# A two-product Strassen-style MLP kernel on one core: x by a plain load, w1 in five chunks, input checks moved, w2 sums made earlier

## The chip, the core and the metric

The kernel runs on one core of a Trainium2 chip. The metric is the time of one execution on the device in microseconds (us). Kernels are compared by the median of several executions, and by a ratio from rounds in which both ran on the same chip. A ratio is the mean time of one kernel's fast runs over that of the other's fast runs of the same rounds, so it is not quite the ratio of the medians that I quote.

Engines have short names in the profile: PE is TensorE (matrix products), PEld its weight loads, DVE is VectorE, ACT is ScalarE, POOL is GpSimd, SP is the engine that only issues DMA.

## The reference

```python
batch, seq, dim, hidden = 16, 256, 512, 2048      # 4096 tokens, all float32
h = x @ w1                                        # w1: 512 x 4096
gate, value = np.split(h, 2, axis=-1)
h = np.maximum(gate, 0) * value
return h @ w2                                     # w2: 2048 x 512
```

## The kernel before

Both products use Winograd's form of Strassen's algorithm: seven half-size products in place of eight, paid for with sums. For the weights the sums are called T1 to T4, for the data S1 to S4. The 4096 tokens are worked through in four sets of 1024. A set has a first product of 16 blocks (128 hidden columns each) and a second product of four token blocks; the tail of one set overlaps the start of the next. Set 0 makes its first two blocks by ordinary products ("plain"), because the sums are not there yet.

The inputs are cast to f16 while they are loaded. That is only safe for inputs of ordinary size, so ScalarE squares and adds up every part of x, w1 and w2 (a "check", `look` in the code), and a verdict at the end (`judge`, `count`) decides whether a slow, general version must run instead.

One block of the first product. TensorE runs P1, P5, P2, P6, P3, P7 and P4, two matmuls each, interleaved with the next block:

```python
def P1(self):
    self.X = psx.tile(...);  self.mm("P1", self.X, True)
    self.Y = psy.tile(...);  nc.scalar.copy(out=self.Y, in_=self.X)     # Y starts as a copy of X
def P5(self):
    self.W = psw.tile(...);  self.mm("P5", self.W, True)
    nc.scalar.activation(self.p5, self.W, COPY, scale=GS)
def P2(self):
    self.mm("P2", self.X, False)              # must wait until ScalarE has read X
def P6(self):
    self.mm("P6", self.Y, False)              # adds to what ScalarE wrote
    nc.scalar.activation(self.u2, self.Y, COPY, scale=GS)
# ... P3: two VectorE ops; P7: one; P4: one, which writes g
```

The start, the checks and the work around the two products:

```python
# start: everything through GpSimd's casting DMA queue
for b in range(0, NB, 2):
    nc.gpsimd.dma_start(out=xn[:, b:b + 2], in_=x_v[0, :, b:b + 2])    # first half of x, f16
fetch_w1(0)                                                            # w1 of blocks 0 and 1
nc.gpsimd.dma_start(out=xn[:, NB:], in_=x_v[0, :, NB:])                # second half
for i in range(1, 6): fetch_w1(i)                                      # w1 in eight chunks
# ... in set 0 GpSimd makes T1 to T4 of w1, pair of blocks by pair of blocks, then all of w2's,
# then w1's of blocks 0 and 1:
if jb // 2 + 1 < NP: w1_ops(jb // 2 + 1)
else:                w2_ops(); w1_ops(0)
# checks: two of x in a block, or one of w1 (sets 1, 2), or two of x and one of w2 (set 3)
at_block(s, (4 if s == 0 else i // (2 * NB)) + i // 2, look_x)
at_block(1 + i // NP, 8 + i % NP, look_w1);  at_block(3, 1 + i, look_w2);  at_block(3, 13, judge)
# ... after set 0's first product, VectorE makes S1, S2, S4, S3 of g, in two halves each
for m in ("S1", "S2", "S4", "S3"):
    for h in (0, NHC // 2): g_sum(nc.vector, go, m, h, h + NHC // 2)
# second product: two token blocks at a time
for b in range(0, NB, 2):
    for name in ("P1", "P2", "P5", "P6", "P3", "P7", "P4"):
        for c in (b, b + 1): yield from step(name, c)
```

## Time and profile before

| | before |
|---|---|
| median time | 344.91 us (344.87 to 345.13, 3 runs) |
| span of the profiled run | 343.8 us |
| first product of block 2 / its last product | 20.0 / 26.3 us |
| period of a block in the first product | 3.02 to 3.06 us without a check, 3.13, 3.23 and up to 4.31 with checks |
| last product of set 0's last block to the last product of set 1's first | 39.5 us |

First the page of the profile: the span, TensorE's row of busy tenths in 40 slices, and the row of its granted clock in tenths.

```profile
span 343.8 us, 5094 instructions
PE   6889999937999998999999998999997777999993
PEclk9999999987999999999999999999999999999998
```

TensorE is the engine that bounds the kernel, with holes at the start, in slices 9 and 10 (69 to 86 us) and in slices 31 to 34 (258 to 292 us). The clock falls where the second hole is.

Who TensorE waited for (us in total, number of waits, the longest):

```profile
PE X L196 <- ACT Y L203: 11.1, 13, 1.1
PE W L270 <- DVE g_S L261: 7.5, 3, 4.4
PE W L196 <- POOL wt L150: 0.7, 2, 0.5
```

Line 196 is a matmul of the first product, line 270 one of the second. The first wait is P2, which adds to X and must wait until ScalarE has copied X to Y. The second is the second product, waiting for the sums of g.

The chain of waits (start, us, what) shows why the copy is late:

```profile
133.38 0.82 ACT sq L183
134.52 0.50 ACT Y L203
135.06 0.59 PE X L196 x2
```

A check (`sq`) sits on ScalarE right before the copy. The start of every block's last product, read from the timeline, gives what this costs. Against 3.045 us a block (the mean period where there is no check), set 0 loses 1.6 us, sets 1 and 2 lose 2.9 us each, set 3 loses 10.0 us.

The hole at 69 to 86 us, in the timeline of VectorE and of GpSimd (start, us for all, engine, line, operation, output and input, count):

```profile
68.70 7.19 DVE L261 TENSOR_TENSOR g_S<-g 128x2048 f16<-128x2048 f16 x2
75.82 4.26 DVE L261 TENSOR_TENSOR g_S<-g_S,g 128x2048 f16<-128x2048 f16 x2
80.00 4.26 DVE L261 TENSOR_TENSOR g_S<-g,g_S 128x2048 f16<-128x2048 f16 x2
84.19 2.35 DVE L261 TENSOR_TENSOR g_S<-g 128x2048 f16<-128x2048 f16 x2
```

```profile
69.78 5.04 POOL L153 TENSOR_TENSOR v_T<-w_sb,v_T 128x2048 f16<-128x2048 f16 x1
...
81.05 2.13 POOL L150 TENSOR_TENSOR wt<-wr,wt 128x512 f16<-128x512 f16 x1
```

Four pairs of the same size take 7.2, 4.3, 4.3 and 2.35 us. GpSimd is summing w2 and w1 until 83.2 us, and only the last pair is free of it. The Trainium skill, "SBUF — State Buffer", section Who interferes with whom, says why: VectorE and GpSimd share one pair of SBUF ports under an exclusive lock, and a VectorE operation with two SBUF inputs and a GpSimd operation that reads SBUF block each other for a whole instruction. The trace agrees: a sum takes 1.2 us when alone, and beside GpSimd 2.1 us (the second and third pair) or 3.6 us (the mean of the first).

### The profile page before, as it was taken

What the parts mean: (1) busy time and instruction counts of PE and PEld (TensorE: products, weight loads), DVE (VectorE), ACT (ScalarE), POOL (GpSimd) and SP (SyncE); (2) the same over time, 40 slices, a digit from 0 to 9 for tenths busy, and PEclk for the clock granted to TensorE, in tenths of its full rate; (3) what the DMA queues carried; (4) which work ended last, traced back from release to release, by engine and by line L of the source; (5) the groups of instructions that cost most, each with busy time, mean ns of one, the idle gap of its engine ahead of it and who ended that gap; (6) DMA issues with size and microseconds to landing.
All of it is one profiled execution on the core that took longest, in us unless ns stands there. A gap on an engine that the chain in (4) does not pass through costs nothing.

```text
span 343.8 us, 5094 instructions
## 1 busy us (share of the span) xinstructions
PE 311.8 (91%) x1847; PEld 179.8 (52%) x1847; DVE 216.0 (63%) x328; ACT 191.3 (56%) x451; POOL 166.4 (48%) x146
## 2 busy tenths in 40 slices
PE   6889999937999998999999998999997777999993
PEld 2433444615884443448874443458873333436883
DVE  1377788899516886885327887784336565798301
ACT  2347786401238678783338778772348888553230
POOL 8499999996001433992001344991001232698000
PEclk9999999987999999999999999999999999999998
DMA  7999994350320100018320200026220100000113
GB/s 97 192 196 200 227 218 95 61 122 2 122 93 31 61 3 0 0 37 152 121 92 33 61 0 0 2 54 169 85 93 31 61 2 0 1 0 3 64 60 129
DMA packets 32541, 25.54 MB, mean 74 GB/s; under 512 B 13728, under 2 KB 28448, under 8 KB 32416
## 3 DMA queue, kind: packets, MB, share of 16 engines
q0 software_dynamic: 11776, 10.49, 19.2%
q1 hardware_dynamic: 20592, 14.62, 14.5%
q8 instruction: 16, 0.26, 0.3%
q14 instruction: 13, 0.11, 0.1%
q10 hardware_dynamic: 144, 0.07, 0.1%
HBM read 24.12 MB, written 11.53 MB: 104 GB/s over the span
## 4 chain that ended last, share of the span: by engine, by line
PE 62%; ACT 13%; DVE 8%; issue 7%; POOL 6%; DMA 3%; ACTq 0%; DVEq 0%; POOLq 0%
PE Y L196 16%; PE X L196 13%; PE Y L270 11%; PE X L270 8%; PE W L196 8%; PE W L270 7%; ACT sq L183 6%; DVE g_S L261 5%; ACT Y L203 4%; POOL wt L150 3%; DMA wr<-in_w_dram 3%; ACT pu L217 2%; POOL wr L337 2%; DVE cc L223 1%; POOL w_sb L431 1%
## 5 line engine op out<-in xcount | busy, mean ns | idle before, releaser
L261 POOL TENSOR_TENSOR g_S<-g 128x512 f16<-128x512 f16 x42 | 48.5, 1155 | 141.7 <-DVE g L233 141.7
L196 PE MATMUL X<-x_A,wr 128*128 128x512 f16 x248 | 73.6, 378 | 11.8 <-ACT Y L203 11.1
L196 PEld LDWEIGHTS <-wt 128*128 128x128 f16 x496 | 48.0, 97 | 59.5 <-POOL wt L150 2.5
L223 DVE SCALAR_TENSOR_TENSOR cc<-W,pu 128x512 f32<-128x512 f32 x62 | 42.8, 691 | 53.1 <-ACT pu L217 52.9
L196 PE MATMUL Y<-x_S,wt 128*128 128x512 f16 x248 | 73.7, 379 | 0.0
L196 PEld LDWEIGHTS <-wr 128*128 128x128 f16 x372 | 36.1, 97 | 60.9 <-issue 24.6
L270 PEld LDWEIGHTS <-g_S 128*128 128x128 f16 x512 | 50.7, 100 | 16.9 <-DVE g_S L261 10.0
L217 ACT ACTIVATE pu<-Y 128x512 f32<-128x512 f32 x62 | 37.0, 597 | 37.5 <-PE Y L196 37.5
L224 DVE SCALAR_TENSOR_TENSOR g<-X,cc 128x512 f16<-128x512 f32 x62 | 42.9, 691 | 2.4
L233 DVE SCALAR_TENSOR_TENSOR g<-Y,cc 128x512 f16<-128x512 f32 x62 | 42.2, 681 | 2.8 <-PE Y L196 2.8
L229 DVE SCALAR_TENSOR_TENSOR cc<-Y,pu 128x512 f32<-128x512 f32 x62 | 42.2, 681 | 0.3 <-PE Y L196 0.2
L203 ACT COPY Y<-X 128x512 f32<-128x512 f32 x62 | 35.9, 578 | 11.1 <-PE X L196 8.6
L270 PEld LDWEIGHTS <-g 128*128 128x128 f16 x384 | 37.5, 98 | 8.3 <-issue 0.2
L196 PE MATMUL W<-x_S,wr 128*128 128x512 f16 x124 | 36.9, 379 | 0.8 <-DVE x_S L178 0.8
L196 PE MATMUL W<-x_S,wt 128*128 128x512 f16 x124 | 36.9, 380 | 0.7 <-POOL wt L150 0.7
L196 PE MATMUL Y<-x_A,wt 128*128 128x512 f16 x124 | 36.9, 379 | 0.7 <-DVE flag L409 0.7
L210 ACT ACTIVATE pu<-W 128x512 f32<-128x512 f32 x62 | 36.6, 590 | 0.7 <-PE W L196 0.7
L270 PE MATMUL Y<-v_T,g_S 128*128 128x256 f16 x256 | 32.1, 279 | 0.9 <-DVE g_S L261 0.9
L299 DVE SCALAR_TENSOR_TENSOR o<-W,pv 128x256 f32<-128x256 f32 x16 | 6.7, 423 | 40.4 <-PE W L270 19.8
L270 PE MATMUL X<-w_sb,g 128*128 128x256 f16 x256 | 30.6, 273 | 0.0
L319 ACT ACTIVATE o<-Y 128x256 f32<-128x256 f32 x15 | 5.7, 379 | 36.0 <-PE Y L270 36.0
L270 PE MATMUL W<-v_T,g_S 128*128 128x256 f16 x128 | 16.7, 287 | 6.0 <-DVE g_S L261 6.0
(62 smaller groups left out, 327.8 us busy)
## 6 DMA issues: line engine op xcount, KB each, us to landing
out_dram<-o SPq DMA_DIRECT2D x31, 256.0 KB, 2.0
wr<-in_w_dram POOLq DMA_DIRECT2D x16, 256.0 KB, 10.2
x<-in_x_dram POOLq DMA_DIRECT2D x3, 1024.0 KB, 14.9
xn<-x SPq DMA_DIRECT2D x6, 512.0 KB, 4.1
w_sb<-in_w_dram POOLq DMA_DIRECT2D x4, 512.0 KB, 9.5
g_S<-in_x_dram POOLq DMA_DIRECT2D x2, 256.0 KB, 5.0
g_S<-in_x_dram POOLq DMA_DIRECT2D x1, 512.0 KB, 8.9
x_A<-x SPq DMA_TRANSPOSE x12, 3.6
```

The source lines that it names most:

```text
L150: turned(lambda n, a, b, o: nc.gpsimd.tensor_tensor(W[n](i), W[a](i), W[b](i), op=o))
L183: nc.scalar.activation(sq, t, SQUARE, scale=(P / of) ** 0.5, accum_out=st[:, at:at + 1])
L196: nc.tensor.matmul(ps, W[wn](self.jb // 2)[:, b, js], self.xo[xn][:, b, :], start=fresh and b == 0, stop=b == 1, skip_group_check=True)
L203: nc.scalar.copy(out=self.Y, in_=self.X)
L210: nc.scalar.activation(self.p5, self.W, COPY, scale=GS)
L217: nc.scalar.activation(self.u2, self.Y, COPY, scale=GS)
L223: nc.vector.scalar_tensor_tensor(out=self.c12, in0=self.W, scalar=GS, in1=self.u2, op0=MULT, op1=ADD)
L224: nc.vector.scalar_tensor_tensor(out=self.g[:, self.jb, :TH], in0=self.X, scalar=0.0, in1=self.c12, op0=MAX, op1=MULT)
L229: nc.vector.scalar_tensor_tensor(out=self.c22, in0=self.Y, scalar=GS, in1=self.p5, op0=MULT, op1=ADD)
L233: nc.vector.scalar_tensor_tensor(out=self.g[:, self.jb, TH:], in0=self.Y, scalar=0.0, in1=self.c22, op0=MAX, op1=MULT)
L261: eng.tensor_tensor(go[n][:, h0:h1], go[i0][:, h0:h1], go[i1][:, h0:h1], op=op)
L270: nc.tensor.matmul(ps, go[gn][:, k, b * P:(b + 1) * P], V[vn][:, k, :], start=fresh and k == 0, stop=k == NHC - 1, skip_group_check=True)
```

## The change

The intent has four parts:

1. Start: the first half of x comes as f32 by a plain DMA on the SP queue, parallel to w1 on GpSimd's queue. TensorE turns it as f32, and the first products go in quarters (256 tokens), so that they can start as soon as half of it is there.
2. w1 comes in five chunks (2, 2, 4, 4, 4 blocks). VectorE makes the T sums of blocks 2 and 3, and later those of blocks 0 and 1.
3. Checks: one short x check per block behind P5, the long ones of w1 and w2 and the verdict inside the second product.
4. Three of the four w2 sums come before the first second product, the fourth on VectorE; three token blocks' P1 and P2 come first.

```diff
-NWARM = 10
+NWARM = 7
+    CHUNKS = ((0, 2), (2, 2), (4, 4), (8, 4), (12, 4))
...
-        for b in range(0, NB, 2):
-            for name in ("P1", "P2", "P5", "P6", "P3", "P7", "P4"):
-                for c in (b, b + 1):
-                    yield from step(name, c)
+        order = [("P1", 0), ("P1", 1), ("P1", 2), ("P2", 0), ("P2", 1), ("P2", 2)]
+        order += [(n, b) for n in ("P5", "P6", "P3", "P7", "P4") for b in (0, 1)]
+        order += [("P1", 3), ("P5", 2), ("P2", 3), ("P5", 3)]
+        order += [(n, b) for n in ("P6", "P3", "P7", "P4") for b in (2, 3)]
+        for i, (n, b) in enumerate(order):
+            for f in BESIDE.get((s, i), ()):
+                f()
+            yield from step(n, b)
...
+    for b in (0, 2):
+        nc.sync.dma_start(out=xf[:, b:b + 2], in_=x_v[0, :, b:b + 2])
+    fetch_w1(0, 0)
+    make_identity(nc, ident[F32])
+    fetch_w1(0, 1)
+    for b in (0, 2):
+        nc.gpsimd.dma_start(out=xh[:, b:b + 2], in_=x_v[0, :, NB + b:NB + b + 2])
...
+    x_sum(xo)                 # S1
+    plain[0].close(1)
+    x_sum(xo)                 # S2
+    w1_one()                  # T1 of blocks 2 and 3, on VectorE
+    plain[1].close(1)
+    w1_one(); x_sum(xo); w1_one(); x_sum(xo); w1_one()      # T2, S4, T3, S3, T4
...
+    LOOKS: x check i at block i (set 0: i + 2, the last three at block 15)
+    BESIDE[s, 7 + 2 * i] = w1 and w2 checks;  BESIDE[3, 3] = judge; [3, 5] = count; [3, 8] = flag
...
+            w1_ops(nc.gpsimd, 4, 2); fetch_w2(0); fetch_w2(1); w1_ops(nc.gpsimd, 6, 2)
+            fetch_w2(2); fetch_w2(3); w1_ops(nc.gpsimd, 8, 2)
+            for c in range(1, NS): cast_x(c)
+            w1_ops(nc.gpsimd, 10, 2); w1_ops(nc.gpsimd, 12, 4)
+            for m in ("T1", "T2", "T3"): w2_op(nc.gpsimd, m)
```

More of the change, by code (lines that the diff above doesn't have):

```diff
@@ L125, in fast_way @@
     out_v = out2.rearrange("(s h b p) n -> s h b p n", p=P, b=NB, h=2)
-    wr = [wpool.tile([P, 4, 2, 2 * P], F16, name=f"wr{i}") for i in range(NP)]
-    wt = [wpool.tile([P, 4, 2, 2 * P], F16, name=f"wt{i}") for i in range(NP)]
+    CHUNKS = ((0, 2), (2, 2), (4, 4), (8, 4), (12, 4))
+    place = {jb + i: (c, i) for c, (jb, n) in enumerate(CHUNKS) for i in range(n)}
+    wr = [wpool.tile([P, 4, 2, n * P], F16, name=f"wr{c}") for c, (_, n) in enumerate(CHUNKS)]
+    wt = [wpool.tile([P, 4, 2, n * P], F16, name=f"wt{c}") for c, (_, n) in enumerate(CHUNKS)]
     w2_sb = wpool.tile([P, NJ, DO], F16, name="w2_sb")
@@ L135, in fast_way, with W, w1_ops, w2_op @@
     st = wpool.tile([P, NW + NJ // 2], F32, name="st")
-    W = {"B11": lambda i: wr[i][:, 0:2, 0], "B21": lambda i: wr[i][:, 2:4, 0],
-         "B12": lambda i: wr[i][:, 0:2, 1], "B22": lambda i: wr[i][:, 2:4, 1],
-         "T1": lambda i: wt[i][:, 0], "T2": lambda i: wt[i][:, 1],
-         "T3": lambda i: wt[i][:, 2], "T4": lambda i: wt[i][:, 3]}
+    def W(name, jb, n=1):
+        c, i = place[jb]
+        raw = {"B11": (0, 0), "B21": (2, 0), "B12": (0, 1), "B22": (2, 1)}
+        js = slice(i * P, (i + n) * P)
+        if name in raw:
+            e, g = raw[name]
+            return wr[c][:, e:e + 2, g, js]
+        return wt[c][:, int(name[1]) - 1, :, js]
     V = {"B11": w2_sb[:, :NHC, :HALF], "B12": w2_sb[:, :NHC, HALF:], "B21": w2_sb[:, NHC:, :HALF], "B22": w2_sb[:, NHC:, HALF:],
          **{n: t for n, t in v_t.items()}}
+    TURNS = (("T1", "B12", "B11", SUB), ("T2", "B22", "T1", SUB), ("T3", "B22", "B12", SUB), ("T4", "B21", "T2", SUB))
     def turned(op):
-        for n, i0, i1, o in (("T1", "B12", "B11", SUB), ("T2", "B22", "T1", SUB), ("T3", "B22", "B12", SUB),
-                             ("T4", "B21", "T2", SUB)):
-            op(n, i0, i1, o)
-    def w1_ops(i):
-        turned(lambda n, a, b, o: nc.gpsimd.tensor_tensor(W[n](i), W[a](i), W[b](i), op=o))
-    def w2_ops():
-        turned(lambda n, a, b, o: nc.gpsimd.tensor_tensor(V[n], V[a], V[b], op=o))
+        for t in TURNS:
+            op(*t)
+    def w1_ops(eng, jb, n):
+        turned(lambda m, a, b, o: eng.tensor_tensor(W(m, jb, n), W(a, jb, n), W(b, jb, n), op=o))
+    def w2_op(eng, name, n=1):
+        for m, a, b, o in TURNS:
+            if m == name:
+                for h in range(0, NHC, NHC // n):
+                    hs = slice(h, h + NHC // n)
+                    eng.tensor_tensor(V[m][:, hs], V[a][:, hs], V[b][:, hs], op=o)
     warm = tmp.tile([P, 2, TH], F32, name="warm", tag="tmp")
@@ L157, in fast_way @@
     nc.vector.memset(warm[:, 0], 0.0)
-    ident = wpool.tile([P, P], F16, name="ident")
+    ident = {t: wpool.tile([P, P], t, name=f"ident{k}") for k, t in enumerate((F32, F16))}
     def idle(n):
@@ L174, in fast_way @@
     SUMS = (("S1", "A21", "A22", ADD), ("S2", "S1", "A11", SUB), ("S4", "A12", "S2", SUB), ("S3", "A11", "A21", SUB))
-    def x_sums(o):
-        for n, i0, i1, op in SUMS:
-            yield nc.vector.tensor_tensor(o[n], o[i0], o[i1], op=op)
     def look(t, at, of):
@@ L193, in mm @@
             wn, xn = WX[name]
-            js = slice(self.jb % 2 * P, self.jb % 2 * P + P)
             for b in range(2):
-                nc.tensor.matmul(ps, W[wn](self.jb // 2)[:, b, js], self.xo[xn][:, b, :],
+                nc.tensor.matmul(ps, W(wn, self.jb)[:, b], self.xo[xn][:, b, :],
                                  start=fresh and b == 0, stop=b == 1, skip_group_check=True)
@@ L238, in __init__, with open, mm, close @@
             self.g, self.jb = g, jb
-        def products(self, h, a1, a2):
-            js = slice(self.jb % 2 * P, self.jb % 2 * P + P)
-            X = psx.tile([P, TH], F32, name="X", tag="X")
-            Wt = psw.tile([P, TH], F32, name="W", tag="W")
-            for a, gate, value in ((a1, "B11", "B12"), (a2, "B21", "B22")):
-                for ps, wn in ((X, gate), (Wt, value)):
-                    for b in range(2):
-                        nc.tensor.matmul(ps, W[wn](self.jb // 2)[:, b, js], a[:, b, :], start=a is a1 and b == 0,
-                                         stop=a is a2 and b == 1)
+        def open(self):
+            self.X = psx.tile([P, TH], F32, name="X", tag="X")
+            self.W = psw.tile([P, TH], F32, name="W", tag="W")
+        def mm(self, side, a, q):
+            ts = slice(q * 256, q * 256 + 256)
+            ps = (self.X, self.W)[side]
+            for e in range(4):
+                name = (("B11", "B21"), ("B12", "B22"))[side][e // 2]
+                nc.tensor.matmul(ps[:, ts], W(name, self.jb)[:, e % 2], a[:, e, ts], start=e == 0, stop=e == 3,
+                                 skip_group_check=True)
+        def close(self, h):
             v = tmp.tile([P, 2, TH], F32, name="v", tag="tmp")[:, 0]
-            nc.scalar.activation(v, Wt, COPY, scale=GS)
-            nc.vector.scalar_tensor_tensor(out=self.g[:, self.jb, h * TH:(h + 1) * TH], in0=X, scalar=0.0,
+            nc.scalar.activation(v, self.W, COPY, scale=GS)
+            nc.vector.scalar_tensor_tensor(out=self.g[:, self.jb, h * TH:(h + 1) * TH], in0=self.X, scalar=0.0,
                                            in1=v, op0=MAX, op1=MULT)
@@ L261, in g_sum @@
                 eng.tensor_tensor(go[n][:, h0:h1], go[i0][:, h0:h1], go[i1][:, h0:h1], op=op)
+    BESIDE = {}
     def mm2_stream(s, go):
@@ L333, in advance, with fetch_w1, fetch_w2, cast_x @@
                 return
-    def fetch_w1(i):
-        for g in range(2):
-            nc.gpsimd.dma_start(out=wr[i][:, :, g], in_=w1_v[:, :, g, i * 2 * P:(i + 1) * 2 * P])
+    def fetch_w1(c, g):
+        jb, n = CHUNKS[c]
+        nc.gpsimd.dma_start(out=wr[c][:, :, g], in_=w1_v[:, :, g, jb * P:(jb + n) * P])
+    def fetch_w2(i):
+        nc.gpsimd.dma_start(out=w2_sb[:, 4 * i:4 * i + 4, :], in_=w2_v[:, 4 * i:4 * i + 4, :])
+    def cast_x(s):
+        nc.gpsimd.dma_start(out=x16[s], in_=x2[s * SET:(s + 1) * SET, :])
     def g_tiles():
@@ L344, in fast_way @@
     g, go = g_tiles()
-    xn = go["S1"]
-    def turn_first(o, h):
-        for b in range(NB):
-            pool, nm = (psx, "X") if b % 2 else (psw, "W")
-            ps = pool.tile([P, 4, P], F16, name=nm, tag=nm)
-            for e in range(4):
-                nc.tensor.transpose(ps[:, e], xn[:, h * NB + b, e * P:(e + 1) * P], ident)
-            copy = nc.scalar.copy if b % 2 else nc.vector.tensor_copy
-            copy(out=o[f"A{h + 1}"][:, :, b * P:(b + 1) * P], in_=ps)
-    for b in range(0, NB, 2):
-        nc.gpsimd.dma_start(out=xn[:, b:b + 2], in_=x_v[0, :, b:b + 2])
@@ L358, in fast_way, with turn_first @@
-    fetch_w1(0)
-    make_identity(nc, ident)
-    nc.gpsimd.dma_start(out=xn[:, NB:], in_=x_v[0, :, NB:])
-    for i in range(1, 6):
-        fetch_w1(i)
+    xf = go["S1"].rearrange("p a t -> p (a t)").bitcast(F32).rearrange("p (b d) -> p b d", b=NB)
+    xh = go["S2"][:, :NB]
+    def turn_first(o, h, b0):
+        if h == 0:
+            for b in (b0, b0 + 1):
+                ps = psy.tile([P, 4, P], F32, name="Y", tag="Y")
+                for e in range(4):
+                    nc.tensor.transpose(ps[:, e], xf[:, b, e * P:(e + 1) * P], ident[F32])
+                copy = nc.scalar.copy if b % 2 else nc.vector.tensor_copy
+                copy(out=o["A1"][:, :, b * P:(b + 1) * P], in_=ps)
+            return
+        ps = psx.tile([P, 4, 2, P], F16, name="X", tag="X")
+        for b in range(2):
+            for e in range(4):
+                nc.tensor.transpose(ps[:, e, b], xh[:, b0 + b, e * P:(e + 1) * P], ident[F16])
+        nc.vector.tensor_copy(out=o["A2"][:, :, b0 * P:(b0 + 2) * P], in_=ps.rearrange("p e b t -> p e (b t)"))
@@ L364, in fast_way, with plain_mm @@
+    for b in (0, 2):
[5 more added lines that the diff above has]
+        nc.gpsimd.dma_start(out=xh[:, b:b + 2], in_=x_v[0, :, NB + b:NB + b + 2])
+    make_identity(nc, ident[F16])
+    for c in range(1, len(CHUNKS)):
+        for g_ in range(2):
+            fetch_w1(c, g_)
     xo = x_tiles()
     plain = [Plain(g, jb) for jb in range(NPLAIN)]
+    def plain_mm(h, q):
+        for side in range(2):
+            for p in plain:
+                p.mm(side, xo[f"A{h + 1}"], q)
@@ L366, in fast_way @@
     idle(NWARM)
-    turn_first(xo, 0)
+    turn_first(xo, 0, 0)
     idle(NFILL)
     for p in plain:
-        p.products(0, xo["A11"], xo["A12"])
-    turn_first(xo, 1)
-    sums = x_sums(xo)
-    next(sums)
-    plain[0].products(1, xo["A21"], xo["A22"])
-    next(sums)
-    plain[1].products(1, xo["A21"], xo["A22"])
-    for _ in sums:
-        pass
-    def look_x(s, i):
-        b = i // 2 if s == 0 else i // 2 % NB
-        look(xn[:, b, i % 2 * 256:i % 2 * 256 + 256], 4 * NB * s + i, 256)
+        p.open()
@@ new lines, in fast_way, with x_sum @@
+    for p in plain:
+        p.mm(0, xo["A1"], 0)
+    turn_first(xo, 0, 2)
+    for p in plain:
+        p.mm(1, xo["A1"], 0)
+    idle(3)
+    plain_mm(0, 1)
+    for p in plain:
+        p.close(0)
+    turn_first(xo, 1, 0)
+    for p in plain:
+        p.open()
+    plain_mm(1, 0)
+    turn_first(xo, 1, 2)
+    plain_mm(1, 1)
+    sums = list(SUMS)
+    def x_sum(o):
+        n, i0, i1, op = sums.pop(0)
+        nc.vector.tensor_tensor(o[n], o[i0], o[i1], op=op)
+    x_sum(xo)
+    plain[0].close(1)
@@ new lines, in fast_way, with w1_one, look_w1 @@
+    x_sum(xo)
+    w1_first = [t for t in TURNS]
+    def w1_one():
+        m, a, b, o = w1_first.pop(0)
+        nc.vector.tensor_tensor(W(m, 2, 2), W(a, 2, 2), W(b, 2, 2), op=o)
+    w1_one()
+    plain[1].close(1)
+    w1_one()
+    x_sum(xo)
+    w1_one()
+    x_sum(xo)
+    w1_one()
+    def look_x(s, i):
+        b = i // 2 % NB
+        t = xn if s else (xf, xh)[i // 2 // NB]
+        look(t[:, b, i % 2 * 256:i % 2 * 256 + 256], 4 * NB * s + i, 256)
+    def look_w1(i):
+        c, o = place[i // 2 * 2]
+        look(wr[c][:, :, i % 2, o * P:(o + 2) * P], NX + i, 1024)
@@ L384, in fetch_rows, with look_w2 @@
+    def look_w2(i):
+        look(w2_sb[:, 2 * i:2 * i + 2].rearrange("p h n -> p (h n)"), NW + i, 1024)
     def fetch_rows(s, h):
@@ L387, in fetch_rows @@
         return t
-    def look_w1(i):
-        look(wr[i // 2][:, :, i % 2], NX + i, 1024)
-    def look_w2(i):
-        look(w2_sb[:, 2 * i:2 * i + 2].rearrange("p h n -> p (h n)"), NW + i, 1024)
     def judge():
@@ L403, in judge @@
             nc.vector.tensor_reduce(out=fit[:, :1], in_=ok, axis=mybir.AxisListType.X, op=ADD)
-        LOOKS[3, 14] = [lambda: count(fit, P * n)]
+        BESIDE[NS - 1, 5] = [lambda: count(fit, P * n)]
     def count(fit, n):
-        ps = psx.tile([P, TH], F32, name="X", tag="X")
+        ps = psw.tile([P, TH], F32, name="W", tag="W")
         nc.tensor.matmul(ps[:1, :1], fit[:, :1], fit[:, 1:], start=True, stop=True)
-        nc.vector.tensor_scalar(out=flag, in0=ps[:1, :1], scalar1=n - 0.5, scalar2=None, op0=LT)
+        BESIDE[NS - 1, 8] = [lambda: nc.vector.tensor_scalar(out=flag, in0=ps[:1, :1], scalar1=n - 0.5, scalar2=None,
+                                                             op0=LT)]
     LOOKS = {}
-    def at_block(s, jb, f):
-        LOOKS.setdefault((s, jb), []).append(f)
     for s in range(NS):
         for i in range(4 * NB):
-            at_block(s, (4 if s == 0 else i // (2 * NB)) + i // 2, lambda s=s, i=i: look_x(s, i))
-    for i in range(2 * NP):
-        at_block(1 + i // NP, 8 + i % NP, lambda i=i: look_w1(i))
-    for i in range(NJ // 2):
-        at_block(3, 1 + i, lambda i=i: look_w2(i))
-    at_block(3, 13, judge)
-    def fetch_more(i):
-        if i < NP:
-            fetch_w1(i)
-            return
-        i -= NP
-        if i < 4:
-            nc.gpsimd.dma_start(out=w2_sb[:, 4 * i:4 * i + 4, :], in_=w2_v[:, 4 * i:4 * i + 4, :])
-        elif i < 4 + NS - 1:
-            s = i - 3
-            nc.gpsimd.dma_start(out=x16[s], in_=x2[s * SET:(s + 1) * SET, :])
+            LOOKS[s, min(i + 2, NJ - 1) if s == 0 else i] = [lambda s=s, i=i: look_x(s, i)] + (
+                LOOKS.get((s, NJ - 1), []) if s == 0 and i > NJ - 3 else [])
+    for s in range(NS - 1):
+        for i in range(8):
+            f = (lambda i=i + 8 * s: look_w1(i)) if s < 2 else (lambda i=i: look_w2(i))
+            BESIDE[s, 7 + 2 * i] = [f]
+    BESIDE[NS - 1, 3] = [judge]
+    verdict = []
+    BESIDE[NS - 1, 14] = [lambda: verdict.append(nc.values_load(
+        flag[0:1, 0:1], min_val=0, max_val=1, skip_runtime_bounds_check_because="a comparison wrote it"))]
     prev = None
@@ L438, in fast_way @@
     BY_DVE = 2
-    queued = 6
     for s in range(NS):
@@ L448, in fast_way @@
         if s == 0:
-            w1_ops(1)
+            w1_ops(nc.gpsimd, 4, 2)
+            fetch_w2(0)
+            fetch_w2(1)
+            w1_ops(nc.gpsimd, 6, 2)
+            fetch_w2(2)
+            fetch_w2(3)
+            w1_ops(nc.gpsimd, 8, 2)
+            for c in range(1, NS):
+                cast_x(c)
+            w1_ops(nc.gpsimd, 10, 2)
+            w1_ops(nc.gpsimd, 12, 4)
+            for m in ("T1", "T2", "T3"):
+                w2_op(nc.gpsimd, m)
         for at in range(first * PERIOD, last + PERIOD):
@@ L452, in fast_way @@
                 jb, n = plan[at]
-                if s == 0 and n == "P5" and jb % 2 == 0:
-                    for _ in range(3):
-                        fetch_more(queued)
-                        queued += 1
-                    if jb // 2 + 1 < NP:
-                        w1_ops(jb // 2 + 1)
-                    else:
-                        w2_ops()
-                        w1_ops(0)
+                if n == "P1" and s and jb == 4:
+                    late = fetch_rows(s, 1)
+                if n == "P1" and s and jb == 8:
+                    xn = late
                 getattr(blocks[jb], n)()
-                if n == "P1" and s and jb == 4:
-                    xn = fetch_rows(s, 1)
-                if n == "P6":
+                if n == "P5":
                     for f in LOOKS.get((s, jb), ()):
@@ L481, in fast_way @@
                     g_sum(nc.vector, go, m, h, h + NHC // 2)
+            w2_op(nc.vector, "T4", 2)
         else:
@@ L493, in fast_way @@
             advance(stream, 100)
-            for _ in x_sums(xo):
-                pass
+            sums = list(SUMS)
+            for _ in SUMS:
+                x_sum(xo)
+            if s == 0:
+                w1_ops(nc.vector, 0, 2)
             advance(stream, MM2 - TAIL - 100 - done)
         else:
-            unfit = nc.values_load(flag[0:1, 0:1], min_val=0, max_val=1,
-                                   skip_runtime_bounds_check_because="a comparison wrote it")
             advance(stream, MM2)
         prev = stream
-    return unfit
+    return verdict[0]
 _INS = ['x', 'w1', 'w2']
```

## The prediction

> **What bounds the kernel now.** TensorE, between a few holes. In the timeline its matmuls start every 0.215 us (128x512) or 0.109 us (128x256): 62 blocks of 14 and 896 of the second product make about 285 us of 344. The rest:
> - Start: the first product of block 2 starts at 20.0 us; before it TensorE waits for x (5.3, 8.4 us) and w1 (10.4 us).
> - Block period (starts of each block's last product): 3.02 to 3.06 us without a check on ScalarE, 3.13 with two short x checks (0.41 + 0.19 us each), 3.23 with one long check (0.82 or 1.06 + 0.19), 4.31 with three. Against 3.04, set 0 loses 1.6 us (0.7 of it waits for GpSimd's w1 sums), sets 1 and 2 2.9 each, set 3 10.0 (verdict matmul included). The chain of waits names ScalarE's square, then the Y copy.
> - Set 0 to 1: VectorE's sums of g run from 68.7 to 86.5 us, 7.2 us for the first pair, 4.3 for the next two, 2.35 for the last, while GpSimd makes the w2 sums and w1 sums. The Trainium skill ("SBUF — State Buffer", Who interferes with whom) says that a two-SBUF-input VectorE op and a reading GpSimd op exclude each other; the last pair, at 1.2 us an op, agrees. TensorE loses about 12 us from 64.9 to 89.7. The granted clock falls to half for 6.8 us here; the skill ("TensorE: Matmul & The Clock Gate", The HAM clock gate) puts it down to idling, and the 4.4 us wait just before agrees.
>
> **What changes, on the critical path.**
> 1. Checks: x one per block behind P5, where ScalarE has a gap of 0.59 us; w1, w2 and the verdict in the second product, where ScalarE has room (eight 1.25 us checks in 14 us, tight but buffered). Gain: 2.7 + 2.7 in sets 1 and 2, 9.7 in set 3, 0.7 in set 0.
> 2. w2 sums before the first second product: three of four on GpSimd before it, one on VectorE (2 x 0.7 us). Sums then about 4 x 2.35 + 1.4 us, and three blocks' P1/P2 instead of two fill TensorE meanwhile. Gain about 8.8, less 1.0 because the last block of set 0 gets three checks: 7.8. The half clock should vanish.
> 3. Larger w1 chunks: the 0.7 us of GpSimd waits goes.
> 4. Start: x lands earlier over the SP queue (estimate 5 and 6.5 us). But f32 transposes, 11 fillers, and VectorE, which must close both first-half blocks before it copies the second half, eat it. Block 2's P1 anywhere from 17 to 22 us. Net gain about 0.5, +-3.
>
> Sum: 2.7 + 2.7 + 9.7 + 0.7 + 7.8 + 0.7 + 0.5, about 24.8.
>
> **Predicted: 320.0 us, 8 in 10 between 315 and 327.** Faster by over 2%: 0.96; within 2%: 0.03; slower: 0.01.
>
> **What would show it.** Step 1: block periods 3.02 to 3.08 in all sets. Step 2: VectorE's 128x2048 sums at 1.2 us, TensorE idle under 6 us between the last block of set 0 and the fourth token block; clock 1.0. Step 3: no TensorE wait for GpSimd's w1 sums. Step 4: the start of block 2.
>
> **What would make it wrong.** Slow f32 transposes or a TensorE left cold by the shorter warm-up (+3); GpSimd, later than thought, stalling blocks 4 to 13 or still running w2 sums under VectorE's (+4); ScalarE backlog in the second product stalling TensorE (+1 per set); x arriving far earlier (-3).

## More of the kernel before

The experiments ran in three groups on three chips, and the kernel before had medians of 345.09, 345.61 and 345.05 us there, so a difference of medians between groups can be off by half a microsecond; the ratios are the fairer comparison.

VectorE's S sums of x take 0.68 or 0.69 us, except the one that starts just after a GpSimd sum of w1 (TensorE waits 0.85 us for it):

```profile
21.40 1.15 POOL L150 TENSOR_TENSOR wt<-wr,wt 128x512 f16<-128x512 f16 x1
21.47 1.63 DVE L178 TENSOR_TENSOR x_S<-x_A,x_S 128x1024 f16<-128x1024 f16 x1
```

## The result, and the profile after

The median is **331.88 us** (330.76 to 333.90, 4 runs) against 344.89 us, a ratio of 0.963 (0.958 to 0.969). The kernel is faster by 3.7%. The prediction said 320.0 and 315 to 327: the direction was right, but about half of the forecast gain is missing.

The profiled run is the slowest of the four (span 332.0 us). Its page:

```profile
span 332.0 us, 5158 instructions
PE   8756999999799999999999999999999999997993
PEclk9998999999999999999999999999999999998997
```

The holes of before are closed: slices 31 to 34 are full now, and of the hole between set 0 and set 1 a small one is left in slice 11 (83 to 91 us). But the third and fourth slices (17 to 33 us) are emptier, and the clock falls there and near the end, not in the change from set 0 to set 1.

TensorE's waits:

```profile
PE Y L203 <- DVE cc L236: 4.0, 5, 1.3
PE W L203 <- DVE wt L439: 3.1, 1, 3.1
PE X L256 <- DVE x_A L384: 2.5, 2, 1.7
PE W L479 <- DVE fit L474: 2.1, 1, 2.1
```

The waits for ScalarE's copy and for the sums of g are gone from the top (the sums of g have 0.7 us left), and four others stand there, all of them on VectorE. Where the time went, by the starts of the blocks' last products in the two traces:

| stretch | before, us | after, us | won | predicted |
|---|---|---|---|---|
| start of the program to block 2's last product | 26.26 | 33.29 | -7.0 | +0.5 |
| set 0, block 2 to block 14 | 38.16 | 36.49 | +1.7 | +1.4 |
| block 14 of set 0 to block 0 of set 1 | 42.59 | 34.47 | +8.1 | +7.8 |
| set 1, block 0 to 15 | 48.56 | 46.71 | +1.9 | +2.7 |
| set 2, block 0 to 15 | 48.56 | 46.73 | +1.8 | +2.7 |
| set 3, block 0 to 15 | 55.71 | 46.68 | +9.0 | +9.7 |
| set 1 to 2, and set 2 to 3 (both) | 55.66 | 54.92 | +0.7 | 0 |
| last block to the end | 28.35 | 32.71 | -4.4 | 0 |
| sum | 343.85 | 332.00 | +11.9 | +24.8 |

So the two main gains came. Two stretches lost what nobody had asked them to lose, and sets 1 to 3 each fell 0.7 to 0.9 us short.

**The start.** TensorE's timeline, at the first product of block 2, its P5 and its last product (idle time before it and its releaser in brackets):

```profile
20.73 0.59 PE L203 MATMUL X<-x_A,wr 128*128 128x512 f16 x2
24.38 0.96 PE L203 MATMUL W<-x_S,wt 128*128 128x512 f16 x2 [3.05 <-DVE wt L439]
...
33.29 0.59 PE L203 MATMUL Y<-x_A,wt 128*128 128x512 f16 x2 [1.31 <-DVE cc L236]
```

Block 2 starts 0.7 us later than before (20.03 us), but takes 12.6 us from its first to its last product instead of 6.2. VectorE's timeline in that time (`x_S` are the S sums of x, `wt` the T sums of w1):

```profile
18.97 0.69 DVE L430 TENSOR_TENSOR x_S<-x_A 128x1024 f16<-128x1024 f16 x1
...
21.73 1.30 DVE L430 TENSOR_TENSOR x_S<-x_S,x_A 128x1024 f16<-128x1024 f16 x1
22.95 1.37 DVE L439 TENSOR_TENSOR wt<-wr 128x512 f16<-128x512 f16 x1
...
24.84 0.77 DVE L439 TENSOR_TENSOR wt<-wr,wt 128x512 f16<-128x512 f16 x1
25.54 1.64 DVE L430 TENSOR_TENSOR x_S<-x_A,x_S 128x1024 f16<-128x1024 f16 x1
27.10 1.37 DVE L439 TENSOR_TENSOR wt<-wr 128x512 f16<-128x512 f16 x1
28.39 1.63 DVE L430 TENSOR_TENSOR x_S<-x_A,x_A 128x1024 f16<-128x1024 f16 x1
29.94 1.37 DVE L439 TENSOR_TENSOR wt<-wr,wt 128x512 f16<-128x512 f16 x1
```

The S sum at 18.97 us takes 0.69 us; another of the same size at 25.54 us takes 1.64 us. GpSimd's first w1 sum starts between the two, at 20.10 us:

```profile
20.10 1.15 POOL L158 TENSOR_TENSOR wt<-wr 128x512 f16<-128x512 f16 x1 [6.88 <-DMA wr<-in_w_dram]
```

**Set 0 to set 1.** VectorE's sums of g, the same pairs as before, with the last w2 sum behind them:

```profile
74.75 2.35 DVE L272 TENSOR_TENSOR g_S<-g 128x2048 f16<-128x2048 f16 x2
77.02 2.35 DVE L272 TENSOR_TENSOR g_S<-g_S,g 128x2048 f16<-128x2048 f16 x2
...
83.83 1.28 DVE L165 TENSOR_TENSOR v_T<-w_sb,v_T 128x1024 f16<-128x1024 f16 x2
```

All four pairs take 2.35 us now. GpSimd finished its last sum at 65.3 us, before any of them.

**Sets 1 to 3.** All periods are 3.02 to 3.06 us but one: block 8 takes 4.1 us. ScalarE's timeline in set 1:

```profile
124.05 0.60 ACT L217 ACTIVATE pu<-W 128x512 f32<-128x512 f32 x1
125.98 0.42 ACT L191 ACTIVATE sq<-xn 128x256 f16<-128x256 f16 x1 [1.33 <-DMA xn<-x]
126.40 0.58 ACT L224 ACTIVATE pu<-Y 128x512 f32<-128x512 f32 x1
```

The check of block 8 is the first of the second x half, and it waits for the load of that half.

**The end.** TensorE's timeline in the last second product:

```profile
299.73 2.35 PE L283 MATMUL X<-w_sb,g 128*128 128x256 f16 x20
304.22 0.16 PE L479 MATMUL W<-fit 128*1 128x1 f16 x1 [2.15 <-DVE fit L474]
304.31 1.86 PE L283 MATMUL X<-w_sb,g 128*128 128x256 f16 x8
305.97 2.81 PE L283 MATMUL W<-v_T,g_S 128*128 128x256 f16 x16
```

The verdict's one-column matmul waits 2.15 us for VectorE, and the products behind it run at half pace: eight take 1.86 us, where eight took 1.04 us elsewhere in this kernel. The clock records show half clock from 304.4 to 307.8 us.

### The profile page after: what moved, and what is told of

It is laid out like the page before. It is cut to its first block, busy times and chain, and to the rows that moved or that the text cites. A ratio compares the mean times of both kernels' runs of the same rounds, so it can differ in the third digit from the quotient of the medians.

```text
span 332.0 us, 5158 instructions
## 1 busy us (share of the span) xinstructions
PE 309.3 (93%) x1879; PEld 184.7 (56%) x1879; DVE 217.8 (66%) x338; ACT 187.5 (56%) x449; POOL 144.3 (43%) x128
## 4 chain that ended last, share of the span: by engine, by line
PE 81%; DVE 11%; ACT 2%; issue 2%; DMA 2%; DVEq 0%; ACTq 0%
PE Y L203 22%; PE X L203 14%; PE W L203 14%; PE Y L283 11%; PE W L283 8%; PE X L283 6%; DVE g_S L272 3%; PE Y L175 2%; DVE x_S L430 1%; DVE wt L439 1%; DVE cc L230 1%; DMA xn<-x 1%; PE X L256 1%; DVE g L240 1%; DVE cc L236 1%
## 5 line engine op out<-in xcount | busy, mean ns | idle before, releaser
L217 ACT ACTIVATE pu<-W 128x512 f32<-128x512 f32 x62 | 37.4, 602 | 3.3 <-PE W L203 3.3
L283 PE MATMUL X<-w_sb,g 128*128 128x256 f16 x256 | 32.2, 277 | 0.0
L283 PE MATMUL Y<-v_T,g_S 128*128 128x256 f16 x256 | 30.9, 273 | 0.4 <-DVE g_S L272 0.4
L191 ACT ACTIVATE sq<-xn 128x256 f16<-128x256 f16 x48 | 19.9, 415 | 4.0 <-DMA xn<-x 4.0
L272 POOL TENSOR_TENSOR g_S<-g_S,g 128x512 f16<-128x512 f16 x18 | 20.8, 1156 | 1.4
```

Source lines behind the costliest of these rows:

```text
L191: nc.scalar.activation(sq, t, SQUARE, scale=(P / of) ** 0.5, accum_out=st[:, at:at + 1])
L272: eng.tensor_tensor(go[n][:, h0:h1], go[i0][:, h0:h1], go[i1][:, h0:h1], op=op)
L283: nc.tensor.matmul(ps, go[gn][:, k, b * P:(b + 1) * P], V[vn][:, k, :], start=fresh and k == 0, stop=k == NHC - 1, skip_group_check=True)
```

## The experiments

The theory has four parts: (a) the start is lost to the port lock, now between VectorE's sums for block 2 and GpSimd's sums for block 4; (b) the end is lost to the verdict's place, and to the half clock that can follow it; (c) block 8 waits for a single-buffered load; (d) the gain between set 0 and set 1 is the same lock, removed. The rivals: VectorE's queue is simply too long; the inputs arrive too late; the half clock comes by itself; block 8 is slow for another reason. All kernels below keep the reference's result unless said otherwise, and each was timed against the kernel before in three rounds. The changed kernel itself is at 331.88 us and a ratio of 0.963; it was not run again in these rounds. The half-width of the 95% interval of a ratio is 0.002 to 0.006, that is 0.7 to 2 us, so gains of 1 to 2 us rest on the traces more than on the times. The diffs below are cut and some of their lines joined.

| run | what is different from the changed kernel | median, us | ratio to before |
|---|---|---|---|
| pool_held | GpSimd's queue reordered | 326.93 | 0.947 |
| turn_on_pool | T sums of blocks 2, 3 on GpSimd | 328.00 | 0.950 |
| count_late | verdict's matmul later | 329.71 | 0.955 |
| looks_shift | first-half x checks one block earlier | 328.94 | 0.952 |
| combined3 | pool_held, count_late, looks_shift | 320.41 | 0.927 |
| x_cast | pool_held, first x half cast by GpSimd's queue | 328.55 | 0.951 |
| sums_back | pool_held, more sums on GpSimd again | 329.75 | 0.956 |
| order_old | pool_held, old order of the second product | 328.77 | 0.951 |
| combined_all | repairs and a reordered start: **wrong result** | 317.93 | 0.919 |
| y_marked | combined_all and three filler matmuls | 318.98 | 0.925 |
| combined_xw | combined_all with other banks | 315.89 | 0.915 |

### pool_held: is it the lock?

```diff
-            w1_ops(nc.gpsimd, 4, 2); fetch_w2(0); fetch_w2(1); w1_ops(nc.gpsimd, 6, 2)
-            fetch_w2(2); fetch_w2(3); w1_ops(nc.gpsimd, 8, 2); cast_x(1); cast_x(2); cast_x(3)
+            for c in range(4): fetch_w2(c)
+            cast_x(1); cast_x(2)
+            w1_ops(nc.gpsimd, 4, 2); w1_ops(nc.gpsimd, 6, 2); w1_ops(nc.gpsimd, 8, 2)
+            cast_x(3)
```

> The changed kernel with GpSimd's queue reordered only: its four w2 fetches and two of the three x casts are issued before its first w1 sum, so that sum should start near 25.5 us instead of 20.1 us, after most of VectorE's seven sums of block 2 and 3 (S2, S4, S3, T1 to T4). VectorE's and TensorE's programs are unchanged. Lock theory (VectorE's two-SBUF-input sums wait for GpSimd's sums, which read SBUF too): those seven fall from 9.45 us in total to about 4, block 2's last product starts near 27 us instead of 33.3, and the time falls by about 6 us to 325. Rival one (VectorE has simply too much queued in front of T1, lock or not): the seven stay near 9 us and the time stays within 1 us. Rival two (the start is late because x, w1 or the f32 transposes come late): block 2's first product stays at 20.7 and so does the time.

Measured: 326.93 us (326.03 to 327.60). Block 2's first product started at 20.70 us, its last at 27.50 us. VectorE's timeline, with its program unchanged:

```profile
21.70 0.68 DVE L430 TENSOR_TENSOR x_S<-x_S,x_A 128x1024 f16<-128x1024 f16 x1
22.30 0.42 DVE L439 TENSOR_TENSOR wt<-wr 128x512 f16<-128x512 f16 x1
...
23.57 0.69 DVE L430 TENSOR_TENSOR x_S<-x_A,x_S 128x1024 f16<-128x1024 f16 x1
24.17 0.42 DVE L439 TENSOR_TENSOR wt<-wr 128x512 f16<-128x512 f16 x1
```

GpSimd's first sum started behind all of them, and block 2's last product came at 27.50 us:

```profile
26.05 1.18 POOL L158 TENSOR_TENSOR wt<-wr 128x512 f16<-128x512 f16 x1
27.50 0.59 PE L203 MATMUL Y<-x_A,wt 128*128 128x512 f16 x2
```

The seven sums took 3.7 us in total instead of 9.45, and block 2's last product came 5.8 us earlier: the sums beside GpSimd account for the whole difference, the half clock that followed TensorE's wait of 3.05 us included. VectorE's queue by itself, and a late arrival of the inputs, are both refuted as the main cause, since neither was touched. That the engines wait for each other, and do not only share a rate, fits the lengths: the short sum (0.42 us) and the long one (0.69 us) both grew by up to the same 0.95 us, to 1.37 and 1.64 us, while a shared rate would stretch the long one more. What is left against the kernel before, 27.50 against 26.26 us, is the part of the start that the lock does not explain.

### turn_on_pool: the same repair from the other side

```diff
-    w1_one(); plain[1].close(1); w1_one(); x_sum(xo); w1_one(); x_sum(xo); w1_one()
+    plain[1].close(1); x_sum(xo); x_sum(xo)
...
+            w1_ops(nc.gpsimd, 2, 2)
             w1_ops(nc.gpsimd, 4, 2)
```

> The changed kernel, but the four w1 sums of blocks 2 and 3 go back from VectorE to GpSimd, ahead of its sums for block 4. GpSimd stands idle from 13.2 to 20.1 us there, and chunk 1 has landed by 14.9 us, so these four should be done near 19.7 us and cost GpSimd nothing. Lock theory: VectorE is left with S2, S4 and S3 beside GpSimd's sums (up to 1.6 us each instead of 0.69), block 2's last product starts near 27.5 us instead of 33.3, the time falls by 5 to 6 us. If VectorE's queue alone were to blame (no lock), the gain would be the four sums at 0.42 us, 1.7 us.

Measured: 328.00 us (325.36 to 329.14), a gain of 3.9 us by the median, below the 5 to 6 that I expected. The profiled run had block 2's last product at 26.72 us, better than expected; the spread of the four runs is wide, and the profiled run had the half clock near the end (297.7 to 301.1 us). GpSimd did the four sums from 14.7 us on, in time in which it stood idle in the changed kernel. VectorE's S sums beside it still took up to 1.70 us, so the lock was there, with fewer operations under it. Block 2's last product came 6.6 us earlier than in the changed kernel, far above the 1.7 us of the queue theory; the times alone, with their spread, would not decide it.

### count_late: the verdict

```diff
-        BESIDE[NS - 1, 5] = [lambda: count(fit, P * n)]
+        BESIDE[NS - 1, 12] = [lambda: count(fit, P * n)]
-        BESIDE[NS - 1, 8] = [flag];  BESIDE[NS - 1, 14] = [verdict]
+        BESIDE[NS - 1, 14] = [flag]; BESIDE[NS - 1, 18] = [verdict]
```

> The changed kernel, but the verdict's matmul stands in front of the second product's step 12 instead of 5, the flag at step 14, its load at step 18. Theory: TensorE waited 2.15 us at this matmul because VectorE must finish the last sums of g before it judges, and the clock then fell to half for 3.4 us because of that wait, costing 1.7 us more. So the wait and the dip at 304 us both go, and the time falls by about 3.5 us. Rival (the dip comes whatever the wait, from the change of product): only 2.1 us are won and a stretch at half clock stays near 300 to 310 us.

Measured: 329.71 us (329.07 to 329.82), 2.2 us less by the median and 4.2 us less than the slowest run of the changed kernel, which was the profiled one. The matmul waits no more:

```profile
306.34 1.91 PE L283 MATMUL W<-w_sb,g_S 128*128 128x256 f16 x16
308.18 0.16 PE L479 MATMUL W<-fit 128*1 128x1 f16 x1
```

There is no half clock in the last second product of its profiled run, and its last stretch takes 28.4 us, as before the change. Whether the half clock follows the wait is open: with a wait of 1.75 to 2.3 us for the verdict still in the program, the profiled runs of turn_on_pool, looks_shift and order_old had it, those of pool_held, x_cast and sums_back did not. So the wait (2.15 us) is in every profiled run with the verdict in that place, and the half clock (3.4 us, an estimated loss of half of that, 1.7 us) in some. That fits the wide spread of the changed kernel's four runs, whose times rise as their mean clock falls (330.76 us at 0.996, 331.00 at 0.989, 332.75 at 0.985, 333.90 at 0.984), and the narrow one here; but the clock is not all of it, for the four runs here stay within 0.75 us at clocks of 0.987 to 0.999. The 3.5 us that I expected is right for a run with the half clock, not for the median.

### looks_shift: block 8

```diff
-        LOOKS[s, ... i] = [look_x(s, i)]
+        LOOKS[s, ... max(i - 1, 0) if i < 8 else i] += [look_x(s, i)]
```

> The changed kernel, but in sets 1 to 3 the eight checks of the first x half stand one block earlier (two in block 0, then one a block to block 6), so that the buffer is free for the second half one block (3 us) earlier. Theory: block 8's period of 4.1 us in sets 1, 2 and 3 is ScalarE waiting for that load, which can start only after block 7's check and takes 4 us. Then block 8 falls to about 3.05 us, block 0 or 1 rises by at most 0.1, and the time falls by about 3 us. Rival (it is the switch to another tile or the GpSimd sums of g that start with block 8): block 8 stays at 4.1.

Measured: 328.94 us (328.37 to 329.36), 2.9 us less. Block 8's period is 3.03 us in all three sets, and blocks 0 to 15 take 45.65 us instead of 46.71. In set 1 the load was issued at 118.3 us instead of 122.0, and the check of block 8 has no wait before it:

```profile
118.33 0.39 SPq L463 DMA_DIRECT2D xn<-x  x1
123.89 0.41 ACT L191 ACTIVATE sq<-xn 128x256 f16<-128x256 f16 x1
```

The rival is refuted: the tile still changes at block 8 and GpSimd's sums still start there.

### combined3: do the repairs add up?

> The three repairs together: GpSimd held back as in the run that reordered its queue, the verdict's matmul at step 12, and the checks of the first x half one block earlier. If the three causes are separate, their gains add up: against the changed kernel 5.0 + 2.2 + 2.9 us by the medians measured one at a time, so about 321.5 to 322; block 2's last product near 27.5 us, no period of 4.1 us, no wait of TensorE for the verdict. If they share a cause (say, the half clock), the sum falls short by 2 us or more.

Measured: 320.41 us (320.00 to 321.07), 11.5 us below the changed kernel, where the three gains one by one sum to 10.1 us. So they are separate causes. The surplus of 1.4 us is no finding: by the ratios, which take out the chip, the three gains are 0.016, 0.009 and 0.011 of the time before, 0.036 in sum, and combined3 has 0.036 (12.5 us). The three together bring the kernel to the time that was predicted for the change; that the two meet so closely is partly luck, for the start still loses 1.4 us where 0.5 was to be won, and other terms make up for it.

### x_cast: what the plain load is worth

```diff
-        nc.sync.dma_start(out=xf[:, b:b + 2], in_=x_v[0, :, b:b + 2])      # f32
+        nc.gpsimd.dma_start(out=xf[:, b:b + 2], in_=x_v[0, :, b:b + 2])    # f16, and f16 transposes
```

> The reordered-queue kernel (GpSimd held back) with one step of the change undone: the first x half comes again as f16 through GpSimd's casting queue, ahead of w1, and is turned as f16. This measures what the plain load of x is worth. By the traces: with it the first product starts at 8.5 us and w1's second quarter lands at 9.7; without it w1 landed at 10.4 and 11.3 before the change. So the first half's products should end about 1.1 us later, block 2's first product near 21.8 instead of 20.7, and the time should be about 1 us longer, 328. If the f32 transposes cost more than the earlier load brings, it is equal or faster, 326 to 327.

Measured: 328.55 us, 1.6 us more than pool_held. TensorE waited 1.4 us for w1's second quarter, and block 2's first product started at 21.96 us. That is 1.3 us later than in pool_held, and by the ratios too the difference is 1.3 us (the medians are from different chips, and the intervals overlap). So the plain load is worth about 1.3 us, f32 transposes paid. The intent was sound; its gain was buried.

### sums_back: the lock at the second site

```diff
-            for m in ("T1", "T2", "T3"): w2_op(nc.gpsimd, m)
+            for m in ("T1", "T2", "T3", "T4"): w2_op(nc.gpsimd, m)
+            w1_ops(nc.gpsimd, 0, 2)
...
-            w2_op(nc.vector, "T4", 2)
...
-                w1_ops(nc.vector, 0, 2)
```

> The reordered-queue kernel with the last w2 sum (T4) and the w1 sums of blocks 0 and 1 given back to GpSimd, so that GpSimd is still summing from 65 to about 75 us while VectorE makes the sums of g from about 69 us. Lock theory at the second site: VectorE's first sums of g take about 2.1 us each instead of 1.2 until GpSimd is done, TensorE idles 2 to 4 us more between set 0 and set 1, although VectorE is spared 2.9 us of work; the time grows by 2 to 4 us over 326.9. Without a lock VectorE would win 1.3 us before the fourth P4 and the time would fall by about 1 us.

Measured: 329.75 us, 2.8 us more than pool_held, although VectorE has less to do. VectorE's sums of g:

```profile
68.37 4.37 DVE L272 TENSOR_TENSOR g_S<-g 128x2048 f16<-128x2048 f16 x2
...
80.08 2.35 DVE L272 TENSOR_TENSOR g_S<-g 128x2048 f16<-128x2048 f16 x2
```

The first pair takes 4.37 us beside GpSimd's sums, the last 2.35 us after GpSimd is done (77.9 us). TensorE's stretch from set 0's last block to set 1's first is 34.4 us instead of 30.7. So the lock is worth 3.7 us of that stretch in this test (3.1 us of the whole by the ratios). It does not go all the way back: before the change GpSimd summed for most of the time in which VectorE made its sums.

### order_old: the three token blocks first

```diff
+        order = [(n, c) for b in (0, 2) for n in ("P1", "P2", "P5", "P6", "P3", "P7", "P4") for c in (b, b + 1)]
```

> The reordered-queue kernel with the second product's order of before (two token blocks at a time) in place of three blocks' P1 and P2 first. The two extra filler steps give TensorE 1.75 us of work while VectorE makes the sums of g, so without them it should idle 1.7 us more between set 0 and set 1 and lose nothing elsewhere: 328.6 us, last product of block 15 to first of the next set 32.4 us instead of 30.7, the other two transitions unchanged at 27.5 us. If the order buys nothing, 326.9.

Measured: 328.77 us, 1.8 us more than pool_held, as expected in sum. It is spread otherwise than I expected: the change from set 0 to set 1 grew by 0.8 us, and the other two by 0.4 and 0.6 us (27.9 and 28.05 instead of 27.5), where I had expected nothing. So the new order also explains the 0.7 us that the change won between the later sets and that nobody had forecast. By the ratios the run is 1.4 us slower, and the intervals overlap.

### combined_all, y_marked, combined_xw: a faster version, and a wrong one

The start is reordered: VectorE copies the first quarter of the second x half before it closes the first half's blocks, ScalarE copies the other quarter, S1, S2, T1, T2 and S4 stand ahead of the closing of the second half, GpSimd issues only its four w2 fetches before its sums, and set 0's three last checks are spread.

```diff
-    for p in plain: p.close(0)
-    turn_first(xo, 1, 0)
-    for p in plain: p.open()
-    plain_mm(1, 0)
-    turn_first(xo, 1, 2)
+    turn_first(xo, 1, 0)          # VectorE copies
+    for p in plain: p.close(0)
+    turn_first(xo, 1, 2)          # ScalarE copies
+    for p in plain: p.open()
+    plain_mm(1, 0)
     plain_mm(1, 1)
+    x_sum(xo); x_sum(xo); w1_one(); w1_one(); x_sum(xo)
+    plain[0].close(1); plain[1].close(1)
+    w1_one(); x_sum(xo); w1_one()
```

> A version meant to beat both: verdict and checks as in the three repairs; VectorE copies the first quarter of the second x half before it closes the first half's blocks, ScalarE copies the other, both through the Y banks; S1, S2, T1, T2 and S4 stand ahead of the closing of the second half; GpSimd issues its four w2 fetches before its first sum (near 20.7 us), no x cast; the three checks of set 0's last block are spread. Theory of the start (TensorE waits 1.7 and 0.8 us for the copy of the second x half, because VectorE closes first, and 1.5 us for T1): block 2's first product moves from 20.7 to about 18.4 us, its last to about 25 us, and the time is 2 to 3 us below the three repairs alone, near 319. If the start is bound by the arrival of w1 or of GpSimd's sums for block 4, TensorE stalls at blocks 4 to 6 instead and the time stays near 321.

Measured: 317.93 us, 2.5 us below combined3, block 2 from 19.39 to 25.43 us; but the result was wrong by a relative error of 0.206. A wrong kernel's time is no result, so two runs settled the cause and mended it.

My suspicion was the state of the PSUM banks. The Trainium skill, "PSUM — Partial Sum Buffer", section The four PSUM rules, says that a matmul which does not clear adds only where TensorE has marked the element as written and overwrites elsewhere, and that ScalarE's writes set no mark. It also says that a transpose of 1- or 2-byte elements, f16 among them, clears the marks of its bank. In this kernel P6 adds to a Y that ScalarE wrote. Combined_all was the first version in which f16 transposes were the last TensorE writes to two Y banks before that; x_cast had them in Y banks too, but with three f32-result fillers behind them, and its result was correct.

```diff
 y_marked:     plain_mm(1, 0)
+    idle(3)                       # one f32-result matmul into each Y bank
     plain_mm(1, 1)
 combined_xw:
-        ps = psy.tile([P, 4, 2, P], F16, name="Y", tag="Y")
+        pool, nm = (psw, "W") if b0 else (psx, "X")
+        ps = pool.tile([P, 4, 2, P], F16, name=nm, tag=nm)
```

> The wrong version again with one addition: three filler f32-result matmuls, which write each of the three Y banks once, between the two quarters of the second half's plain products. If the Y banks were left in a state in which the next matmul overwrites, the fillers mend it and the result is correct; if the fault is a missing wait, a wrong buffer or the ScalarE copy of f16, it stays wrong with the same relative error, 0.206. Time: 0.6 us above the wrong version, 318.5.

> The version meant to beat both, whose result was wrong, with the f16 transposes of the second x half in one X bank and one W bank instead of two Y banks. My reason for the wrong result: blocks 3 and 4 of set 0 start their Y by a ScalarE copy and let the matmul of P6 add to it without clearing; after an f16 transpose as the bank's last TensorE write that matmul overwrites instead of adding. X and W banks always begin with a clearing matmul. So this must be correct, at 318 to 319 us: its second half may wait for one more VectorE step (0.3 us) than the wrong one.

Measured: both are correct. y_marked takes 318.98 us (317.91 to 321.43), and differs from the wrong kernel by the three fillers alone. The fillers also shift the timing, so this alone does not exclude a missing wait; the size of the error does. If P1 is left out of Y in blocks 3 and 4 of set 0, as an overwriting P6 leaves it out, the reference's own inputs give a relative error of 0.20626 in numpy (blocks 2 and 3 would give 0.2075); the chip's was 0.20626. So P6 overwrote in just these two blocks, and the state of the banks is the cause. combined_xw takes **315.89 us** (315.77 to 316.08), a ratio of 0.915 (0.913 to 0.917). It beats both kernels, and it is below the 318 to 319 that I expected. Block 2 goes from 18.09 to 23.37 us there, and TensorE's waits no longer show the copy of the second x half above 0.3 us, the T sum, or the verdict. Part of this is the lock again: VectorE ends its sums there at 21.04 us, before GpSimd's first at 22.04, while in y_marked GpSimd starts at 21.39 and the last two sums take 2.06 and 1.37 us. So the start was bound by the order of the work rather than by the arrival of w1 alone; but combined_all and y_marked did wait 1.0 us for w1 and this run did not, and which of the reordered steps won what is not shown.

## Why the prediction was wrong

**Right.** The mechanism of the checks (step 1): periods are 3.02 to 3.06 us in all sets, apart from block 8 and from set 0's last block with its three checks (3.74), and set 3 won 9.0 of 9.7 us. The w2 sums and the three token blocks (step 2): 8.1 us won where 7.8 were predicted, sums at 1.2 us each, no half clock in that stretch; sums_back and order_old show that both parts of it count. Step 3: no wait for GpSimd's w1 sums is left, though no run shows what the larger chunks alone do. In step 4 the plain load did what it should: x landed at 4.1 and 5.5 us (estimated 5 and 6.5), and x_cast puts its worth at about 1.3 us.

**Wrong: step 4, "Net gain about 0.5, +-3".** The start lost 7.0 us. The prediction named the lock for the sums of g and did not apply it to the other place where the change puts VectorE sums beside GpSimd sums. It followed the start to block 2's first product, 17 to 22 us, which came true (20.73), and put no cost on VectorE's seven sums between that and block 2's last product, although the change moves four sums to VectorE into the very time in which GpSimd starts its own. They took 9.45 us instead of the 3.7 of pool_held, which shows 5.8 of the 7.0 us to be the lock. The other 1.2 us (0.7 us of it is the later first product) fit VectorE's order, which the prediction feared; no run isolates that, but combined_xw, with another order and other copies, reaches block 2's last product at 23.37 us.

**Wrong: the end, a term that the sum left out.** The prediction counted moving the verdict as a gain and did not ask what the verdict waits for in its new place. There it stands behind VectorE's last sums of g in VectorE's program and ahead of most of the second product in TensorE's. The stretch lost 4.4 us in the profiled run: 2.15 us of waiting, and an estimated 1.7 us by a half clock of 3.4 us that comes in some runs; the last 0.5 us went with them in count_late. Count_late won 2.2 us by the median and 3.0 by the ratios.

**Wrong in size: step 1 in sets 1 to 3.** One check per block stretches the first x half over eight blocks, and the second half is loaded into the same buffer. Its load takes 4.0 us and can start only after block 7's check, 3 us before block 8's. That wait, 1.07 us in each set, was not in the sum; looks_shift shows it, with 2.9 us won.

Together these are 7.5 (the start against its forecast), 4.4 and about 3.2 us in the profiled run, 15.1 us; the other terms came 2.2 us better than predicted, in small parts. That is the distance between 24.8 and 11.9. What stays open is why the half clock follows a 2 us wait in some runs and not in others.

## What to carry to other kernels

When work moves to another engine, look at what every engine does in that very time: a sum that takes 0.4 to 1.2 us alone on VectorE took up to 3.3 times as much beside GpSimd's 128x512 sums in these traces, and a lock found at one site must be looked for at every site that the change creates. When a small step (a verdict, a check) is moved off one engine's critical path, ask what it waits for in its new place on every engine that executes it in order. When consumption of a single-buffered tile is spread out, its refill moves with the last reader.

## What the Trainium skill lacked or had wrong

- "SBUF — State Buffer", Who interferes with whom: the lock is as described, but the page gives no times for two streams of sums side by side. Here VectorE's f16 sums of 128x512 rose from 0.42 to 1.37 us and those of 128x1024 from 0.69 to 1.64 us beside GpSimd's 128x512 sums, which themselves rose from 1.15 to at most 1.60 us in the changed kernel.
- "TensorE: Matmul & The Clock Gate", Why this matters for your kernels: the page warns of idle gaps above about 3 us. Here single waits of 1.75 to 2.31 us in dense work (the changed kernel, turn_on_pool, looks_shift, order_old) were followed by 3.4 us of half clock, while waits of 2.1 to 2.2 us in three other runs were not.
- "TensorE: Matmul & The Clock Gate", Part 4: PE-mode transpose: there is no time for f32. In the changed kernel eight f32 transposes of 128x128 took 1.04 us at full clock and 1.92 us at the start, where filler matmuls ran at half pace; eight of f16 took 0.61 us at full clock.
